# Low parts of the down weights by adding DMA transfers, and one order of the SBUF pools

## The chip, the cores and the metric

One core of one Trainium2 chip runs the whole program. The metric is device time in microseconds of one execution; a profile of one execution gives the times of single instructions. The engines are TensorE (PE, with its weight loads as PEld), VectorE (DVE), ScalarE (ACT), GpSimd (POOL) and SyncE (SP). SP, ACT and POOL each issue DMA transfers from a queue of their own; sixteen DMA engines carry them.

## The reference

A decoder trunk with two layers, run for a prompt of 512 tokens and 8 sample tokens that share the weights (D = 1024, fp32):

```python
# every layer
x = x + 0.5 * swiglu_a(rmsnorm(x))
x = x + mixer(rmsnorm(x))      # layer 0: differential attention and gated linear attention
x = x + 0.5 * swiglu_b(rmsnorm(x))   # layer 1's mixer: mLSTM matrix memory
```

A SwiGLU half-step has a gate and an up projection from 1024 to 22 hidden blocks of 128 columns, the product silu(gate) * up, and a down projection back to 1024. There are four half-steps: FFN1, (even mixer), FFN2, FFN3, (odd mixer), FFN4. Besides y the program returns new keys, values and states; the change touches none of these.

## The kernel before

**Data.** x stays in SBUF as 128 partitions by 8 blocks by 520 columns and is worked on in two chunks of 256 and 264 columns. Every fp32 product is made of three matmuls on fp32r operands: `dense` (L86) multiplies high weights by high inputs (L100), high weights by low inputs (L101) and low weights by high inputs (L102). A high part is the rounded copy of a value, the low part what is left.

**Weights.** All weights lie in HBM in the order of their use, in units of eight 128x128 blocks (512 KB). `fetch` (L72) loads a unit into one of three `raw` buffers, from SP's queue, or from POOL's in the even mixer. `split` makes the two parts: ACT copies raw to `whi` (L105) and DVE subtracts, raw minus whi, to `wlo` (L106). `whi` and `wlo` have five buffers each in the half-steps, used as a ring; the mixers have rings of their own (five or seven buffers of half the size). High priority in the framework's scheduler moves the split of a unit ahead of other work. That scheduler fixes the order of instructions on every engine before the program runs.

**A half-step.** `ffn` (L243) takes the 22 hidden blocks in three groups of 8, 7 and 7. The first four of them are plain products; the others use a seven-product scheme with combined weights, whose sums DVE makes (L425). After its hidden blocks each group has a down stage: for each of the eight output blocks as many blocks of down weights as the group has hidden blocks, two chunks (`y`), and DVE's update of x by -0.5 y (L549). A group so has 8 or 7 units of down weights, and the twelve down stages of the four half-steps have 88 (of the 192 casts of whole raw units the others are for gate and up weights). In the third group of FFN1, FFN2 and FFN3 the last four output blocks run chunk by chunk, and the norm of the next step begins beside them. In the mixers `L1510` makes a row `oner`, and the projections' results are `pj`.

**Pools.** SBUF tiles come from pools that lie one above the other and are opened anew for every half-step and mixer; a tile that lies where an older one lay waits until that one has been read for the last time. After a mixer (FFN2, FFN4) the pool `ffn` (xb, the hidden values hh and hl, and others) lies below the weights' pool `whl`; in FFN1 and FFN3 `whl` lies below. Both mixers open their own `whl` first, at the bottom. `xb` holds combined inputs of the seven products and is read for the last time by the last product ahead of the third down stage.

Of the kernel before, what the change touches and what calls it, by code (L numbers as in the profile page):

```python
# [15 lines left out]
P = 128  # L16
D = 1024
KT = 8
# [37 lines left out]
class Net:  # L56
    def __init__(self, nc, tc, t):
        self.nc, self.tc, self.t = nc, tc, t
        self.wq = nc.sync
        self.queue, self.due, self.rate, self.todo, self.side = [], 0.0, STEP, [], []  # L60
        self.seek(0)
# [13 lines left out]
    def weight(self):  # L75
        nc, g = self.nc, self.wgrp
        u, s = divmod(self.wpos, UNIT)
        self.fetch(u)
        v, r = divmod(self.wpos, g)
        if self.hl[0] != v:  # L80
            raw = self.raw[1][:, (s - r) * P:(s - r + g) * P]
            hi = self.whl.tile([P, g * P], F32R, tag="whi", name="whi")
            lo = self.whl.tile([P, g * P], F32R, tag="wlo", name="wlo")
            with self.tc.high_priority(AHF if g == UNIT else AHM):
                self.split(hi, lo, raw)
            self.hl = (v, hi, lo)  # L86
        self.wpos += 1
        return self.hl[1][:, r * P:r * P + P], self.hl[2][:, r * P:r * P + P]
# [118 lines left out]
    def head_norm_steps(self, x, parts, g, s, n, per, js=range(4), y=None):  # L207
# [18 lines left out]
        for j in js:  # L226
# [3 lines left out]
            if m > 1:  # L230
                ex = self.tmp.tile([P, 3, P], F32, tag="ex", name="ex", bufs=1)
# [11 lines left out]
    def ffn(self, pos, first, last, mixed):  # L243
# [10 lines left out]
        from contextlib import ExitStack  # L254
        H = KT // 2
        n0, n1 = CH[0][1], CH[1][1]
        with ExitStack() as ctx:
            self.wgrp = UNIT

            if not mixed:  # L260
                self.whl = self.pool(ctx, "whl", WHL)
            hp = self.pool(ctx, "ffn")
            if mixed:
                self.whl = self.pool(ctx, "whl", WHL)
            pa = self.pool(ctx, "pacc", 6, space=PSUM)
            pst = self.pool(ctx, "pst", 2, space=PSUM)
            self.stat = lambda name: pst.tile([P, 512], F32, tag="st", name=name)
            xh, xl, x = self.xh, self.xl, self.x
            xb = [hp.tile([P, 3, H, n1], F32R, tag=f"xb{i}", name="xb") for i in range(2)]
            late = slice(n0, T)  # L270
            ops = {
                "x11": lambda k: (xh[:, k, :n0], xl[:, k, :n0]),
                "x21": lambda k: (xh[:, H + k, :n0], xl[:, H + k, :n0]),
                "x22": lambda k: (xh[:, H + k, late], xl[:, H + k, late]),
                "a": lambda k: (xh[:, k, late], xl[:, k, late]),
                **{n: lambda k, i=i: (xb[0][:, i, k, :], xb[1][:, i, k, :]) for i, n in enumerate("bcd")},
            }

            slots = {(0, 0): "c", (1, 0): "d", (0, 1): "x22", (1, 1): "b"} if first else \
                {(0, 0): "x11", (1, 0): "x21", (0, 1): "d", (1, 1): "x22"}  # L280

            def put(name, k, n, src):
                hi, lo = ops[name](k)
                self.split(hi[:, :n], lo[:, :n], src)
            xn = hp.tile([P, KT, T], F32, tag="hh", name="xn")
            cm = hp.tile([P, 4, H, n1], F32, tag="hl", name="cm")
            rms = [self.rms, hp.tile([P, n1], F32, tag="rms", name="rms")]

            def raw(c, ks):

                s, n = CH[c]
                for k in ks:
                    q = xn[:, k, s:s + n]
                    g = self.ng[:, self.gi, k:k + 1]
                    if c:
                        nc.scalar.activation(q, x[:, k, s:s + n], AF.Copy, scale=g)
                    else:
                        nc.vector.tensor_scalar(q, x[:, k, s:s + n], g, None, ALU.mult)
                    put(slots[k // H, c], k % H, n, q)

            def norm(c, ks):
                s, n = CH[c]
                for k in ks:
                    q = xn[:, k, s:s + n]
                    r = rms[c]
                    if first:
                        nc.vector.tensor_tensor(out=q, in0=q, in1=r, op=ALU.mult)
                        if c == 0:
                            put("x21" if k >= H else "x11", k % H, n, q)
                    else:  # L310
                        nc.vector.scalar_tensor_tensor(q, x[:, k, s:s + n], self.ng[:, self.gi, k:k + 1], r,
                                                       ALU.mult, ALU.mult)
                        if c == 1:
                            put(slots[k // H, 1], k % H, n, q)

            def scale(c):
                r = self.rn
                self.evict(rms[c], self.spread(lambda b: r[:, b:b + 1], c))

            steps = []  # L320

            def begin():

                lo, hi = slice(0, n0), slice(n0, n1)
                x11, x21 = xn[:, :H, :n0], xn[:, H:, :n0]
                x12, x22 = xn[:, :H, late], xn[:, H:, late]
                a, c, b, d = [cm[:, i] for i in range(4)]
                if first:
                    self.x_stats(0)
                    yield  # L330
                    scale(0)
                    yield
                    raw(1, range(KT))
                    yield
                    for k in range(KT):
                        self.sq_add(1, k)
                    yield
                self.norm_stats(1)
                if not first:
                    norm(0, range(H))  # L340
                yield
                scale(1)
                if first:
                    norm(0, range(H))
                    yield
                norm(1, range(H))
                yield
                norm(1, range(H, KT))
                yield
                nc.vector.tensor_tensor(out=a[:, :, lo], in0=x11, in1=x12[:, :, lo], op=ALU.subtract)  # L350
                nc.vector.tensor_scalar(a[:, :, hi], x12[:, :, hi], -1.0, None, ALU.mult)
                self.split(xh[:, :H, late], xl[:, :H, late], a)
                yield
                norm(0, range(H, KT))
                yield
                nc.vector.tensor_tensor(out=c, in0=x22, in1=x12, op=ALU.subtract)
                nc.vector.scalar_tensor_tensor(b[:, :, lo], c[:, :, lo], -1.0, x11, ALU.mult, ALU.subtract)
                nc.vector.tensor_scalar(b[:, :, hi], c[:, :, hi], -1.0, None, ALU.mult)
                yield
                nc.vector.scalar_tensor_tensor(d[:, :, lo], b[:, :, lo], -1.0, x21, ALU.mult, ALU.subtract)  # L360

            def then():

                a, c, b, d = [cm[:, i] for i in range(4)]
                self.split(xb[0][:, 0], xb[1][:, 0], b)
                yield
                if first:
                    self.split(xh[:, H:, late], xl[:, H:, late], xn[:, H:, late])
                    yield
                self.split(xb[0][:, 1], xb[1][:, 1], c)  # L370
                yield
                self.split(xb[0][:, 2, :, :n0], xb[1][:, 2, :, :n0], d[:, :, :n0])

            def step():
                if steps and next(steps[0], 0) == 0:
                    steps.pop(0)

            def early(f, w, c):

                s, n = CH[c]  # L380
                rhs = lambda k: tuple(q[:, :n] for q in ops[slots[k // H, c]](k % H))
                g, u = bank("g"), bank("u")
                self.dense(g[:, :n], w[:KT], rhs)
                step()
                self.dense(u[:, :n], w[KT + H:] + w[KT:KT + H], rhs)
                step()
                h = f.h[:, s:s + n]
                if first:
                    r = rms[c]
                    v = small("v")[:, :n]  # L390
                    nc.vector.tensor_tensor(out=h, in0=g[:, :n], in1=r, op=ALU.mult)
                    nc.scalar.activation(h, h, AF.Silu)
                    nc.vector.tensor_tensor(out=v, in0=u[:, :n], in1=r, op=ALU.mult)
                    nc.vector.scalar_tensor_tensor(h, v, -1.0, h, ALU.mult, ALU.mult)
                else:
                    nc.scalar.activation(h, g[:, :n], AF.Silu)
# [1451 lines left out]
```

## Time and profile before

| | us |
|---|---|
| median of 3 runs | 2218.35 (2216.83 to 2223.81) |
| profiled execution | 2217.88 |
| its span in the trace | 2216.1 |
| mean granted clock of TensorE | 0.993 of full speed |

The stages in the trace: FFN1 to 375 us, the even mixer to 798, FFN2 to 1158, FFN3 to 1522, the odd mixer to 1850, FFN4 to the end. The down stages stand, among others, at 100 to 148 and 2057 to 2099. In a row of a timeline the square bracket gives how long the engine had been idle before, and what ended that.

### The profile page before, as it was taken

To read this page: it belongs to the slowest core of one execution; us is meant where nothing else is said; L and a number is where in the kernel's file an instruction comes from. 1 tells how busy PE (TensorE), PEld (TensorE's weight loads), DVE (VectorE), ACT (ScalarE), POOL (GpSimd) and SP (SyncE) were. 2 spreads that over 40 slices of the span, in tenths; PEclk is the share of its full clock that TensorE was granted. 3 is DMA by queue.
4 is the path that set the end of the run, shared out by engine and by line. 5 is a ranking of instruction groups with operands and counts; after the bars stand their busy time and mean duration, and the time that the engine had idled before them with its cause. 6 is when DMAs were issued, how large, how long until landed. Compare 5 with 4: busy or idle time off the path is not lost. (4 is left out here: it accounts for less than half of the span.)

```text
span 2216.1 us, 45677 instructions
## 1 busy us (share of the span) xinstructions
PE 2171.6 (98%) x18340; PEld 2047.6 (92%) x18340; DVE 1511.2 (68%) x3161; ACT 1010.1 (46%) x1932; POOL 47.5 (2%) x112
## 2 busy tenths in 40 slices
PE   8999999999999999999999999999999999999999
PEld 8999999876777799999999999999999899999999
DVE  8858585544486697585868767677655678758583
ACT  6526263334523355253635445353555555526261
POOL 0000001000000100000000000000000000000000
PEclk9999999999999999999999999999999999999999
DMA  5323234478677743233223323232545464323322
GB/s 183 105 67 123 78 96 152 137 257 272 235 262 244 236 144 102 81 98 102 83 96 99 124 69 123 71 109 96 157 150 158 149 194 150 96 86 92 110 77 87
DMA packets 107019, 296.30 MB, mean 134 GB/s; under 512 B 12129, under 2 KB 16786, under 8 KB 106678
## 3 DMA queue, kind: packets, MB, share of 16 engines
q1 hardware_dynamic: 93504, 254.91, 36.0%
q0 software_dynamic: 7536, 25.42, 3.6%
q10 hardware_dynamic: 5766, 13.05, 1.6%
q8 instruction: 144, 2.36, 0.4%
q14 instruction: 69, 0.57, 0.1%
HBM read 276.22 MB, written 17.11 MB: 132 GB/s over the span
## 5 line engine op out<-in xcount | busy, mean ns | idle before, releaser
L105 ACT CAST whi<-raw 128x512 fp32r<-128x512 f32 (+1 forms) x440 | 351.1, 806 | 426.5 <-PE y L101 167.1
L106 DVE TENSOR_TENSOR wlo<-raw,whi 128x512 fp32r<-128x512 f32 (+1 forms) x440 | 401.5, 920 | 146.4 <-ACT whi L105 134.8
L100 PE MATMUL y<-hh,whi 128*128 128x256 f32 (+1 forms) x1408 | 398.1, 283 | 0.0
L101 PE MATMUL y<-hl,whi 128*128 128x256 f32 (+1 forms) x1408 | 398.0, 283 | 0.0
L102 PE MATMUL y<-hh,wlo 128*128 128x256 f32 (+1 forms) x1408 | 396.8, 282 | 0.0
L101 PEld LDWEIGHTS y<-hl,whi 128*128 128x128 f32 x1408 | 265.2, 188 | 1.0 <-DVE hl L106 0.7
L100 PEld LDWEIGHTS y<-hh,whi 128*128 128x128 f32 x1408 | 264.7, 188 | 0.8
L102 PEld LDWEIGHTS y<-hh,wlo 128*128 128x128 f32 x1408 | 264.8, 188 | 0.0
L100 PE MATMUL pj<-xh,whi 128*128 128x264 f32 (+1 forms) x896 | 260.8, 291 | 4.1 <-DVE oner L1510 1.5
L102 PE MATMUL pj<-xh,wlo 128*128 128x264 f32 (+1 forms) x896 | 255.1, 285 | 3.0 <-DVE wlo L106 2.9
L101 PE MATMUL pj<-xl,whi 128*128 128x264 f32 (+1 forms) x896 | 256.0, 286 | 0.0
L100 PE MATMUL A<-xb,whi 128*128 128x264 f32 (+1 forms) x864 | 249.3, 290 | 0.6
L101 PE MATMUL A<-xb,whi 128*128 128x264 f32 (+1 forms) x864 | 244.2, 284 | 0.0
L102 PE MATMUL A<-xb,wlo 128*128 128x264 f32 (+1 forms) x864 | 243.0, 284 | 0.1
L105 ACT CAST whi<-graw 128x1024 fp32r<-128x1024 f32 x144 | 147.6, 1049 | 162.7 <-PE y L101 104.1
L549 DVE SCALAR_TENSOR_TENSOR x<-y,x 128x256 f32<-128x256 f32 (+1 forms) x192 | 81.8, 426 | 180.7 <-PE y L102 180.2
L106 DVE TENSOR_TENSOR wlo<-graw,whi 128x1024 fp32r<-128x1024 f32 x144 | 172.4, 1218 | 30.6 <-ACT whi L105 30.6
L100 PEld LDWEIGHTS pj<-xh,whi 128*128 128x128 f32 x896 | 170.5, 190 | 20.1 <-issue 11.2
L102 PEld LDWEIGHTS pj<-xh,wlo 128*128 128x128 f32 x896 | 170.3, 190 | 4.5 <-DVE wlo L106 3.4
L101 PEld LDWEIGHTS pj<-xl,whi 128*128 128x128 f32 x896 | 170.4, 190 | 3.9 <-issue 3.3
L100 PEld LDWEIGHTS A<-xb,whi 128*128 128x128 f32 x864 | 162.5, 188 | 9.2 <-DVE c L476 2.8
L100 PE MATMUL E<-xh,whi 128*128 128x264 f32 x576 | 163.7, 284 | 1.6 <-ACT whi L105 1.6
(468 smaller groups left out, 5093.1 us busy)
## 6 DMA issues: line engine op xcount, KB each, us to landing
raw<-w SPq DMA_DIRECT2D x240, 512.0 KB, 3.6
graw<-w SPq DMA_DIRECT2D x72, 512.0 KB, 4.3
kt<-ckt SPq DMA_DIRECT2D x128, 256.0 KB, 4.4
vtile<-cv SPq DMA_DIRECT2D x128, 256.0 KB, 4.0
raw<-w POOLq DMA_DIRECT2D x40, 512.0 KB, 4.7
cs<-sc SPq DMA_DIRECT2D x16, 512.0 KB, 6.4
kb<-kqd SPq DMA_DIRECT2D x16, 512.0 KB, 6.6
o_cs<-cs ACTq DMA_DIRECT2D x16, 512.0 KB, 5.6
```

The source lines that it names most:

```text
L100: nc.tensor.matmul(ps, lhsT=wh, rhs=xh, start=(ends[0] and i == ks[0]), stop=False, skip_group_check=open_)
L101: nc.tensor.matmul(ps, lhsT=wh, rhs=xl, start=False, stop=False, skip_group_check=open_)
L102: nc.tensor.matmul(ps, lhsT=wl, rhs=xh, start=False, stop=(ends[1] and i == ks[-1]), skip_group_check=open_)
L105: self.nc.scalar.copy(out=hi, in_=src)
L106: self.nc.vector.tensor_tensor(out=lo, in0=src, in1=hi, op=ALU.subtract)
L549: nc.vector.scalar_tensor_tensor(xs, y[:, :n], -0.5, xs, ALU.mult, ALU.add)
```

## The change

In the down stages the low part is made in another way: ACT copies raw to `whi`, ACT writes the negated `whi` to `wlo`, and a DMA transfer from POOL's queue adds the unit from HBM onto it. DVE's subtraction is left out there. All other weights are split as before.

All half-steps use one order of pools: `xb` at the bottom, then `whl`, then `ffn`. FFN2 and FFN3, which follow each other, share the pools and so the ring of weight buffers. Two constant rows move from a pool that lives through the program to the even mixer's own, with their memset.

```diff
@@ weight()
             with self.tc.high_priority(AHF if g == UNIT else AHM):
-                self.split(hi, lo, raw)
+                if g == UNIT and self.wadd:
+                    nc.scalar.copy(out=hi, in_=raw)
+                    nc.scalar.activation(lo, hi, AF.Copy, scale=-1.0)
+                    nc.gpsimd.dma_start(out=lo, in_=self.t["w"][u].bitcast(F32R), accum_op=ALU.add)
+                else:
+                    self.split(hi, lo, raw)
@@ ffn()
-    def ffn(self, pos, first, last, mixed):
+    def ffn(self, steps):
         with ExitStack() as ctx:
             self.wgrp = UNIT
-            if not mixed:
-                self.whl = self.pool(ctx, "whl", WHL)
+            xp = self.pool(ctx, "ffnx")
+            self.whl = self.pool(ctx, "whl", WHL)
             hp = self.pool(ctx, "ffn")
-            if mixed:
-                self.whl = self.pool(ctx, "whl", WHL)
...
+            for pos, first, last, nxt in steps:
+                self.nxt, self.nxk = nxt
+                self.half_step(pos, first, last, xp, hp, pa)
@@ half_step(), the former body of ffn()
-            xb = [hp.tile([P, 3, H, n1], F32R, tag=f"xb{i}", name="xb") for i in range(2)]
+        xb = [xp.tile([P, 3, H, n1], F32R, tag=f"xb{i}", name="xb") for i in range(2)]
...
                 self.seek((fs[0].u0 + 2 * nf) * UNIT)
+            self.wadd = True
...
+            self.wadd = False
@@ even()
             self.ev = ev = self.pool(ctx, "ev")
+            self.rows = [ev.tile([P, 384], F32, tag=f"row{c}", name="row") for c in range(2)]
+            for a in self.rows:
+                nc.gpsimd.memset(a, 1.0)
@@ head_norm_steps()
-                ex = self.tmp.tile([P, 3, P], F32, tag="ex", name="ex", bufs=1)
+                ex = self.ev.tile([P, 3, P], F32, tag="ex", name="ex")
@@ setup()
-        self.rows = [self.tmp.tile([P, 384], F32, tag=f"row{c}", name="row", bufs=1) for c in range(2)]
-        for a in [self.acc[1]] + self.rows:
-            nc.gpsimd.memset(a, 1.0)
+        nc.gpsimd.memset(self.acc[1], 1.0)
```

## Rows read from the trace of the kernel before

**Rows 1.** Page, part 1: busy time and instructions of each engine.

```profile
PE 2171.6 (98%) x18340; PEld 2047.6 (92%) x18340; DVE 1511.2 (68%) x3161; ACT 1010.1 (46%) x1932; POOL 47.5 (2%) x112
```

**Rows 2.** Windows of the down stages, one and the sum of twelve.

```profile
core 0: us, PE busy (x) PEld busy (x) DVE busy (x) ACT busy (x) POOL busy (x), PEclk, DMA share, GB/s
...
2057.00:2099.00 42.00, 42.00 (x350) 41.75 (x349) 24.19 (x40) 9.88 (x13) 0.00 (x0) 1.00 0.28 89
...
sum 525.00, PE 524.97 PEld 521.37 DVE 278.37 ACT 122.17 POOL 10.61; mean PE 43.75 PEld 43.45 DVE 23.20 ACT 10.18 POOL 0.88
```

**Rows 3.** Window of a last product before its down stage.

```profile
2042.00:2058.00 16.00, 15.89 (x132) 15.68 (x131) 13.84 (x22) 10.72 (x19) 0.00 (x0) 1.00 0.41 142
```

**Rows 4.** Timeline of PE, FFN1 to the even mixer: start, us, instruction.

```profile
374.61 0.28 PE L102 MATMUL y<-hh,wlo 128*128 128x264 f32 x1
375.63 0.39 PE L100 MATMUL pj<-xh,whi 128*128 128x256 f32 x1 [0.75 <-ACT whi L105]
375.86 0.28 PE L101 MATMUL pj<-xl,whi 128*128 128x256 f32 x1
379.00 0.58 PE L102 MATMUL pj<-xh,wlo 128*128 128x256 f32 x1 [2.86 <-DVE wlo L106]
```

**Rows 5.** Timelines of ACT and DVE there.

```profile
374.97 0.61 ACT L105 CAST whi<-raw 128x512 fp32r<-128x512 f32 x1
...
377.57 0.43 DVE L106 TENSOR_TENSOR xl<-xt,xh 128x256 fp32r<-128x256 f32 x1
...
378.26 1.29 DVE L106 TENSOR_TENSOR wlo<-raw,whi 128x512 fp32r<-128x512 f32 x2
```

**Rows 6.** Windows there, columns as in rows 2.

```profile
378.00:384.00 6.00, 5.00 (x23) 4.99 (x24) 5.46 (x23) 0.91 (x3) 1.07 (x2) 0.50 0.89 282
...
385.00:386.00 1.00, 1.00 (x10) 0.88 (x8) 0.00 (x0) 0.85 (x3) 0.00 (x0) 1.00 0.98 401
```

**Rows 7.** Timeline of PE, the waits at the other three borders.

```profile
1159.41 0.39 PE L100 MATMUL g<-xh,whi 128*128 128x256 f32 x1 [1.04 <-ACT whi L105]
...
1160.36 0.39 PE L100 MATMUL u<-xh,whi 128*128 128x256 f32 x1 [0.45 <-ACT whi L105]
...
1523.12 0.39 PE L100 MATMUL pj<-xh,whi 128*128 128x256 f32 x1 [0.56 <-ACT whi L105]
...
1525.09 0.39 PE L100 MATMUL pj<-xh,whi 128*128 128x256 f32 x1 [1.46 <-DVE oner L1510]
...
1851.56 0.39 PE L100 MATMUL g<-xh,whi 128*128 128x256 f32 x1 [1.13 <-ACT whi L105]
...
1852.51 0.39 PE L100 MATMUL u<-xh,whi 128*128 128x256 f32 x1 [0.45 <-ACT whi L105]
```

**Rows 8.** Groups by shape: busy us, mean ns, idle before.

```profile
L106 DVE TENSOR_TENSOR wlo<-raw,whi 128x1024 fp32r<-128x1024 f32 x192 | 232.7, 1221 | 41.4 <-ACT whi L105 41.1
...
L105 ACT CAST whi<-raw 128x1024 fp32r<-128x1024 f32 x192 | 199.2, 1047 | 235.5 <-PE y L101 129.4 <-DVE raw L425 60.3 <-issue 16.5
...
L1462 ACT ACTIVATE cs<-cs,pdb 128x512 f32<-128x512 f32 x32 | 22.5, 720 | 42.5 <-DMA cs<-sc 38.9 <-issue 3.5
```

**Rows 9.** DMA queues, issues with us to landing, and POOL's group of issues.

```profile
q1 hardware_dynamic: 93504, 254.91, 36.0%
...
raw<-w POOLq DMA_DIRECT2D x40, 512.0 KB, 4.7
...
o_k<-kn POOLq DMA_DIRECT2D x1, 1040.0 KB, 8.8
...
L72 POOL DMA_DIRECT2D raw<-w x40 | 21.2, 529 | 622.1 <-DMA raw<-w 331.0 <-DVE wlo L106 237.8 <-ACT xh L105 11.9
```

**Rows 10.** Timelines of ACT and PE around the start of FFN4's second down stage.

```profile
2047.59 2.00 ACT L105 CAST whi<-raw 128x1024 fp32r<-128x1024 f32 x2
...
2049.81 0.37 ACT L577 ACTIVATE c<-A 128x256 f32<-128x256 f32 x1
...
2054.71 1.05 ACT L105 CAST whi<-raw 128x1024 fp32r<-128x1024 f32 x1 [0.21 <-PE B L101]
...
2057.80 0.28 PE L102 MATMUL y<-hh,wlo 128*128 128x256 f32 x1
```

More of the change, by code (lines that the diff above doesn't have):

```diff
@@ L240, in head_norm_steps @@
             nc.vector.scalar_tensor_tensor(xs, xs, g(j), bc[:, :n], ALU.mult, ALU.mult)
-    def ffn(self, pos, first, last, mixed):
-        nc, tc = self.nc, self.tc
+    def ffn(self, steps):
         from contextlib import ExitStack
-        H = KT // 2
-        n0, n1 = CH[0][1], CH[1][1]
         with ExitStack() as ctx:
             self.wgrp = UNIT
-            if not mixed:
-                self.whl = self.pool(ctx, "whl", WHL)
+            xp = self.pool(ctx, "ffnx")
+            self.whl = self.pool(ctx, "whl", WHL)
             hp = self.pool(ctx, "ffn")
-            if mixed:
-                self.whl = self.pool(ctx, "whl", WHL)
             pa = self.pool(ctx, "pacc", 6, space=PSUM)
@@ L267, in ffn @@
             self.stat = lambda name: pst.tile([P, 512], F32, tag="st", name=name)
-            xh, xl, x = self.xh, self.xl, self.x
-            xb = [hp.tile([P, 3, H, n1], F32R, tag=f"xb{i}", name="xb") for i in range(2)]
[L270 to L287, printed above, removed]
@@ L289, in raw @@
-            def raw(c, ks):
-                s, n = CH[c]
[L292 to L296, printed above, removed]
-                    else:
[L298 to L396, printed above, removed]
-                    nc.vector.scalar_tensor_tensor(h, u[:, :n], -1.0, h, ALU.mult, ALU.mult)
@@ L399, in unit @@
-            def unit(u, gate):
-                raw = (hp.tile([P, UNIT * P], F32, tag="graw", name="graw", bufs=2) if gate else
-                       self.wraw.tile([P, UNIT * P], F32, tag="raw", name="raw"))
-                self.wq.dma_start(out=raw, in_=self.t["w"][u])
-                return raw
-            def parts(src, n, names):
-                tag = "" if n == 2 else "u"
-                hi = self.whl.tile([P, n * H * P], F32R, tag=f"whi{tag}", name="whi", bufs=None if n == 2 else 2)
-                lo = self.whl.tile([P, n * H * P], F32R, tag=f"wlo{tag}", name="wlo", bufs=None if n == 2 else 2)
-                self.split(hi, lo, src)
-                return {name: [(hi[:, i * P:i * P + P], lo[:, i * P:i * P + P]) for i in range(b * H, b * H + H)]
-                        for b, name in enumerate(names)}
@@ L414, in weights_gate @@
-            def weights_gate(f):
-                f.g = unit(f.u0, True)
-                with tc.high_priority(AHF):
-                    f.w = parts(f.g, 2, ("g1", "g2"))
-            def weights_rest(f):
-                B = H * P
-                f.u = unit(f.u0 + 1, False)
-                g1, g2, u2, u1 = f.g[:, :B], f.g[:, B:], f.u[:, :B], f.u[:, B:]
-                def add(x, y):
-                    nc.vector.tensor_tensor(out=x, in0=x, in1=y, op=ALU.add)
-                with tc.high_priority(AHF):
-                    f.w |= parts(u2, 1, ("u2",))
-                    add(u2, u1)
-                    add(u1, g1)
-                    f.w |= parts(f.u, 2, ("s1", "s3"))
-                    add(g1, u2)
-                    add(g2, g1)
-                    f.w |= parts(f.g, 2, ("s2", "s4"))
@@ L435, in ffn @@
-            class Hidden:
-                def __init__(self, u0):
-                    self.u0 = u0
-            def bank(name):
-                return pa.tile([P, 512], F32, tag="acc", name=name)
-            def small(name):
-                return hp.tile([P, n1], F32, tag=name, name=name, bufs=2)
-            def product(kind, f, j):
-                w, v = {"p1": ("g1", "x11"), "p2": ("g2", "x21"), "q5": ("s1", "a"), "q6": ("s2", "b"),
-                        "p7": ("s3", "c"), "p3": ("s4", "x22"), "p4": ("u2", "d")}[kind]
-                n = n0 if kind in ("p1", "p2", "p4") else n1
-                new = kind in ("p1", "p2", "q5")
-                if kind == "p1":
-                    f.A = bank("A")
-                elif kind == "p2":
-                    f.B = bank("B")
-                elif kind == "q5":
-                    f.E = bank("E")
-                ps = f.B if kind == "p2" else f.E if kind in ("q5", "p3") else f.A
-                self.dense(ps[:, :n], f.w[w], lambda k: tuple(q[:, :n] for q in ops[v](k)), ends=(new, True),
-                           open_=kind != "p2")
-                if kind == "p1":
-                    f.c1 = small("c1")
-                    self.evict(f.c1[:, :n0], ps[:, :n0])
-                elif kind == "p2":
-                    g = f.c1[:, :n0]
-                    nc.vector.tensor_tensor(out=g, in0=ps[:, :n0], in1=g, op=ALU.add)
-                    nc.scalar.activation(g, g, AF.Silu)
-                elif kind == "q5":
-                    f.c5 = small("c5")
-                    self.evict(f.c5, ps[:, :n1])
-                elif kind == "q6":
-                    f.v = small("v")
-                    self.evict(f.v, ps[:, :n1])
-                elif kind == "p3":
-                    nc.vector.tensor_tensor(out=f.v, in0=ps[:, :n1], in1=f.v, op=ALU.add)
-                    nc.scalar.activation(f.v, f.v, AF.Silu)
-                elif kind == "p7":
-                    nc.vector.tensor_tensor(out=f.c5, in0=ps[:, :n1], in1=f.c5, op=ALU.add)
-                    nc.vector.tensor_tensor(out=f.v, in0=f.v, in1=f.c5, op=ALU.mult)
-                    self.split(hh[:, j, late], hl[:, j, late], f.v)
-                elif kind == "p4":
-                    g = f.c1[:, :n0]
-                    nc.vector.tensor_tensor(out=g, in0=ps[:, :n0], in1=g, op=ALU.mult)
-                    self.split(hh[:, j, :n0], hl[:, j, :n0], g)
-                step()
@@ L485, in ffn @@
-            u0 = pos // UNIT
-            groups = []
-            for nf in GROUPS:
-                groups.append([Hidden(u0 + 2 * j) for j in range(nf)])
-                u0 += 3 * nf
-            leads = groups[0][:LEAD]
-            self.seek(pos)
-            if first:
-                self.fetch(pos // UNIT)
-                self.x_load(0, KT)
-                raw(0, range(KT))
-            steps.append(begin())
-            i = 0
-            while i < LEAD:
-                fs = leads[i:i + (2 if i == 0 else 1)]
-                ws = [self.weights(2 * KT) for _ in fs]
-                if first and i == 0:
-                    self.x_load(KT, 2 * KT)
-                for f in fs:
-                    f.h = hp.tile([P, T], F32, tag="h", name="h", bufs=LEAD)
-                if i == 0 and not first:
-                    step()
-                for c in range(2):
-                    for f, w in zip(fs, ws):
-                        early(f, w, c)
-                i += len(fs)
@@ L511, in ffn @@
-            while steps:
-                step()
-            steps.append(then())
-            for gi, (nf, fs) in enumerate(zip(GROUPS, groups)):
-                order = []
-                for j in range(LEAD if gi == 0 else 0, nf):
-                    order += [("gate", j), ("rest", j), ("p1", j), ("q5", j)] + [("p4", j - 1)] * (j > (LEAD if gi == 0 else 0))
-                    order += [("q6", j), ("p2", j), ("p3", j), ("p7", j)]
-                order.append(("p4", nf - 1))
-                hh = hl = None
-                for kind, j in order:
-                    if hh is None and kind in ("p7", "p4"):
-                        hh = hp.tile([P, max(GROUPS), T], F32R, tag="hh", name="hh")
-                        hl = hp.tile([P, max(GROUPS), T], F32R, tag="hl", name="hl")
-                        if gi == 0:
-                            for i, f in enumerate(leads):
-                                self.split(hh[:, i], hl[:, i], f.h)
-                    if kind == "gate":
-                        weights_gate(fs[j])
-                    elif kind == "rest":
-                        weights_rest(fs[j])
-                    else:
-                        product(kind, fs[j], j)
-                while steps:
-                    if next(steps[0], 0) == 0:
-                        steps.pop(0)
-                self.seek((fs[0].u0 + 2 * nf) * UNIT)
-                end = gi == len(GROUPS) - 1
-                def hrhs(c):
-                    s, n = CH[c]
-                    return lambda k: (hh[:, k, s:s + n], hl[:, k, s:s + n])
-                def down(d, c, w):
-                    s, n = CH[c]
-                    y = bank("y")
-                    self.dense(y[:, :n], w, hrhs(c))
-                    xs = x[:, d, s:s + n]
-                    nc.vector.scalar_tensor_tensor(xs, y[:, :n], -0.5, xs, ALU.mult, ALU.add)
-                    if end:
-                        if last:
-                            if c == 1:
-                                nc.sync.dma_start(out=self.t["o_y"][:, d, :], in_=x[:, d, :])
-                        else:
-                            self.sq_add(c, d)
-                if end:
-                    self.gi = self.nxt
-                lag = 4 if (end and not last) else 0
-                for d in range(KT - lag):
-                    w = self.weights(nf)
-                    down(d, 0, w)
-                    down(d, 1, w)
-                if lag:
-                    ahead = self.norm_lead() if self.nxk == "ffn" else self.norm_ahead(1)
-                    w = [self.weights(nf) for _ in range(lag)]
-                    for c in range(2):
-                        for i in range(lag):
-                            down(KT - lag + i, c, w[i])
-                            if c:
-                                next(ahead, None)
-                    for _ in ahead:
-                        pass
@@ L1657, in run @@
             self.setup(ctx)
-            for i, st in enumerate(stages):
-                last = i == len(stages) - 1
-                self.nxt, self.nxk = (None, None) if last else (stages[i + 1][1], stages[i + 1][0])
-                if st[0] == "ffn":
-                    self.ffn(st[2], i == 0, last, i > 0 and stages[i - 1][0] != "ffn")
-                else:
-                    getattr(self, st[0])(*st[2:])
-                    if last:
+            nxt = [(st[1], st[0]) for st in stages[1:]] + [(None, None)]
+            last = len(stages) - 1
+            i = 0
+            while i <= last:
+                self.nxt, self.nxk = nxt[i]
+                if stages[i][0] == "ffn":
+                    j = i
+                    while i < last and stages[i + 1][0] == "ffn":
+                        i += 1
+                    self.ffn([(stages[k][2], k == 0, k == last, nxt[k]) for k in range(j, i + 1)])
+                else:
+                    getattr(self, stages[i][0])(*stages[i][2:])
+                    if i == last:
                         self.nc.sync.dma_start(out=self.t["o_y"], in_=self.x)
+                i += 1
             self.x_close()
```

279 lines of the change are left out of this document (added).

## The prediction

> **What bounds the kernel now.** I read the engines' shares first: PE 98% of the span, no other engine above 68% [rows 1]. So only two kinds of edit can move the time: one that makes PE idle, and one that removes an idle stretch of PE. Next come the windows. The change rewrites the twelve down stages, so their table tells what there is to win in them: in 525 us of them PE is busy for 524.97, DVE for 278 and ACT for 122 [rows 2]. No time is to be won there; 42 us hold 350 matmuls, 0.12 us each, so a unit (8 blocks, 2 chunks, 3 products, 48 matmuls) lasts 5.76 us. The last product before a down stage costs PE a tenth of a microsecond at most: 15.89 of 16, with DVE at 13.84 and ACT at 10.72, the fullest place of both [rows 3]. Then PE's timeline at the borders of half-steps and mixers: there PE does stand still, and always for the first weights of the next stage or what follows from them [rows 4, 7]. That is what the new order of pools touches.
>
> **The borders (order of pools): a gain.** A matmul follows the one before by 0.12 us; where PE waited, the step between starts is the shown idle time plus 0.27, so each wait costs its idle time plus 0.15.
>
> *FFN1 to the even mixer.* The last y starts at 374.61, the first pj at 375.63, its second product at 375.86 and its low-part product at 379.00: (1.02 - 0.12) + (3.14 - 0.12) = 3.9 us [rows 4]. ACT casts the first mixer weights only at 374.97, directly after the last y, because the mixer's weight buffers lie where FFN1's weights and hidden values lay; DVE is then late with the low part as it has the norm's work in its queue [rows 5]. After this idle time the granted clock is 0.50, the lower level, from 378 to 384, and back to 1.00 at 385: 23 matmuls took 5.00 us, 0.217 each instead of 0.12, another 2.2 us [rows 6]. Together 6.1. With the new order these buffers lie over xb, last read by the last product, a whole down stage earlier, so cast and low part can be made ahead. What is late next is the norm: its last xl ends at 378.00, and the eighth block's second product would want it 22 matmuls after 374.73, at 377.4: 0.6 stays. Gain 5.5.
>
> *FFN2 to FFN3* now share one ring of weight buffers. Idle 1.04 + 0.45 [rows 7], plus 0.15 each: 1.8. I take it all, as the ring's next buffer comes free with every down unit.
>
> *FFN3 to the odd mixer.* Idle 0.56 for the cast and 1.46 for DVE's oner, which is no weight [rows 7]. The first goes (0.7); of the second (1.6) I take half, since the mixer's first low parts are then no longer in DVE's queue beside it. 1.5.
>
> *Odd mixer to FFN4.* Idle 1.13 + 0.45, 1.9 with the restarts [rows 7]. The buffers will lie over early-released tiles, not over yl, which the last matmul reads; but casts are then queued between the projection's own work on ACT, so I take 1.2.
>
> *Even mixer to FFN2* waits for other things; nothing. The moved memset of the rows is two short POOL instructions; nothing.
>
> Sum 5.5 + 1.8 + 1.5 + 1.2 = 10.0. Bounds: 12.1 if every wait goes (6.1 + 1.8 + 2.3 + 1.9), 3 if only about a quarter does, because the raw transfer or DVE's norm takes each wait's place.
>
> **The adds: what is removed.** 88 subtractions of 1221 ns, 107 us of DVE [rows 8]. DVE was idle for nearly half of these stages [rows 2], so this is worth nothing by itself.
>
> **The adds: what is added.** On ACT 88 negations. The nearest row is the cast of the same shape, 1047 ns; a scaled activation of half the size took 720 [rows 8] where the cast took 0.61 us [rows 5], so 1.05 to 1.24. I take 1.05, since it too is one pass over 128x1024: 92 us, ACT 122 to about 214 of 525 in these stages. On POOL 88 issues of 529 ns, 47 us on an engine that is busy for 47 in all [rows 1, 9]. An add waits for its negation, and POOL takes its queue in order: behind it stand only the next adds, and at the end of FFN1 the even mixer's first raw loads, which wait for buffers themselves [rows 9] and are needed a down stage later; so a late add delays nothing but its own unit. SP's raw loads wait for less than before, since a raw buffer is free after ACT's cast instead of after DVE's subtraction. On the DMA engines 88 transfers of 512 KB that read, add and write. No row shows such a transfer.
> Latency: a plain 512 KB transfer from POOL's queue lands after 4.7 us, one of 1040 KB after 8.8 [rows 9]. That gives 4.7 below and 8.7 above (two plain passes in a row, roughly the larger one). I take 6.3: the plain one and one more pass at the engines' rate. A pass is worked out from SP's queue: 254.91 MB in 36.0% of 2216.1 us is 320 GB/s, 1.64 us for 512 KB [rows 9].
> Engine time: with raw's one pass (0.28 of 5.76 is 1.6 [rows 2]) 4.1 us per unit are left, 2.5 passes. One pass is the lower bound; three (read, read, write, one after the other) the upper. I take the middle, two, 3.3 us: hidden, with the engines busy for about 0.85 of a down stage.
> The Trainium skill, "Collectives: The Full Stack", section "The bandwidth ceiling: the fold count and why AG ≠ RS ≠ AR", says that an add on the way costs no cycles of its own but needs two source reads, and so runs at half the rate (32.35 against 62.28). No run here shows it; by that rule the add would take an estimated 3.3 us here and the sum would stay as it is.
>
> **The first unit of a down stage.** Units later on have time: the third's cast starts at 2054.71 [rows 10] and it is used two units after the first, at 2069: 14.6 us, less 2.1 on ACT, less 6.3. The first has least. Its cast and the second's run from 2047.59 to 2049.59; its low part is read at 2057.80 [rows 10]; the other eleven stages look alike. With negations between, the first negation ends at 2049.7 (cast, negation) or 2050.6 (both casts first). The add lands at 2056.0 to 2056.9 by my value, in time by 0.9; by the upper bound at 2059.3, 1.5 late. Then the evictions on ACT behind these: c<-A at 2049.81 starts 2.1 later, and PE can want its bank. PE has other banks and products, so I take 0.25 us per stage, between 0 and the full 2.1: 12 x 0.25 = 3.0, at most 25. Below zero is possible too: DVE, at 13.84 of 16 here, loses two subtractions per transition, and PE's 0.11 us of idle time could go, 12 x 0.11 = 1.3 us.
>
> **Sum.** Profiled execution 2217.9 (span 2216.1 and 1.8 around it) - 10.0 + 3.0 = 2210.9. The median of the runs is 2218.35, half a microsecond more; I say 2211.
>
> **Rivals.**
> *Late at each transition:* the adds land after the first use, or ACT's evictions hold PE up, 0.5 to 1.6 us each: 12 x 0.5 to 1.6 gives 6 to 19, so 2207.9 + 6 to 19: 2214 to 2227. For it: 0.9 us of slack by my value, and a full ACT and DVE exactly there [rows 3, 10]. Against: PE has the whole of two more products in between.
> *The add is slow, and the kernel slower:* if an add takes the 16 engines more than 4.1 us (2.5 passes), units can't arrive at PE's rate. At three passes a unit takes 4 x 1.64 = 6.56 instead of 5.76 us: 88 x 0.80 = 70, time 2208 + 70 = 2278; at four, 88 x 2.44 = 215, 2423. For it: nothing in the trace prices a transfer that reads its target. Against: rows of plain transfers leave 0.72 of the engines free.
> *The borders don't gain:* buffers free earlier, but casts keep their place in ACT's order, or raw and DVE's norm are last: 3 gained and 3 lost, 2218 (2215 to 2221). For it: an engine's order is fixed beforehand, and two of the four waits come partly from DVE. Against: the casts follow directly on the last y, so what held them was the buffer.
> *More is gained:* all 12.1, nothing at the transitions, and some of DVE's lateness at FFN starts goes: 2201 to 2207.
>
> **How the numbers follow.** Forecast (2207 to 2213) 0.40; late at transitions 0.22; slow add 0.15; borders don't gain 0.10; more gained 0.13. A measurement of this kernel tells 0.3% from no change, 6.65 us: 2211.7 to 2225.0 is "same". The forecast lies with 0.34 below and 0.06 in it; more gained is faster; late is 0.15 same and 0.07 slower; borders 0.08 and 0.02; slow add 0.15 slower. Faster 0.34 + 0.13 = 0.47; same 0.06 + 0.15 + 0.08 = 0.29; slower 0.07 + 0.02 + 0.15 = 0.24. Range 2204 to 2230: it leaves out the slow add (0.15), and the ends of more gained and late (0.05). The likeliest case's own range is 2207 to 2213.
>
> **What would show it.** Borders: whi casts for the first mixer and FFN weights ahead of the last y; no idle 2.86 before pj's low product; clock 1.00 through 378 to 384. Adds: DVE near 1404, ACT near 1102 and POOL near 94 us; the POOL add's landing between 4.7 and 8.7; DMA share of a down stage near 0.85. Transitions: no wait of y L102 on a DMA. I am wrong if y L102 waits on wlo's DMA inside the down stages (slow add), if it does for the first unit alone, or if new waits stand at 375, 1159, 1523 and 1851.

## The result: slower by 0.9%

| | us |
|---|---|
| before, median of 6 runs | 2219.01 |
| changed, median of 6 runs | 2239.32 (2236.33 to 2247.56) |
| ratio, with its 95% interval | 1.0092 [1.0078, 1.0105] |
| profiled execution of the changed kernel | 2247.56, span 2245.8, clock 0.989 |

The forecast was 2211, range 2204 to 2230: the measured time lies above it, and it moved the other way. The profiled execution is the slowest of the six; its span is 29.7 us longer than the one of before.

The page's first part, and its rows on queues and issues (packets, MB and share of 16 engines; KB and us to landing):

```profile
PE 2176.8 (97%) x18340; PEld 2054.8 (91%) x18340; DVE 1410.5 (63%) x3073; ACT 1090.1 (49%) x2020; POOL 123.7 (6%) x200
...
q1 hardware_dynamic: 93504, 254.91, 35.0%
q0 software_dynamic: 20208, 71.56, 14.7%
...
wlo<-w POOLq DMA_DIRECT2D x88, 512.0 KB, 9.0
...
raw<-w POOLq DMA_DIRECT2D x40, 512.0 KB, 4.6
```

The work moved as counted: DVE lost 101 us against [rows 1], ACT gained 80, POOL 76, and PE does the same matmuls. The new row is the add's landing, 9.0 us in the median. PE's waits (us in all, times, longest) name it:

```profile
PE y L109 <- DMA wlo<-w: 20.2, 13, 3.6
...
PE ss L161 <- DVE acc L130: 7.4, 2, 3.9
...
PE A L107 <- ACT c L590: 1.3, 8, 0.2
```

The first row has thirteen waits: one at the first unit of each of the twelve down stages (0.3 to 2.7 us, 16.6 in all) and one at FFN1's last unit (3.6). With 0.15 for each restart they cost 22.2 us. After the four longest (2.1 to 3.6 us) the granted clock falls to 0.50, the lower level, for part of the windows below. One of three windows of that kind, and FFN1's (columns as in [rows 2]):

```profile
1014.00:1018.00 4.00, 4.00 (x22) 4.00 (x22) 0.89 (x3) 0.93 (x2) 0.87 (x1) 0.57 1.06 287
...
368.00:374.00 6.00, 4.97 (x29) 4.97 (x30) 1.27 (x3) 0.44 (x2) 0.53 (x1) 0.72 0.31 107
```

(1 - 0.57) x 4 is 1.7 us, three times, and (1 - 0.72) x 6 another 1.7: 6.8. Together 29.0 of the 29.7. All the rest, borders and mixers with their gains and losses, sums to under 1 us.

**The start of a down stage**, the place of [rows 10]. ACT, POOL, SP and PE there:

```profile
2075.04 1.99 ACT L88 CAST whi<-raw 128x1024 fp32r<-128x1024 f32 x2
2076.94 2.00 ACT L89 ACTIVATE wlo<-whi 128x1024 fp32r<-128x1024 f32 x2
```

```profile
2078.28 1.81 POOL L90 DMA_DIRECT2D wlo<-w  x2 [85.92 <-ACT wlo L89]
```

```profile
2075.16 2.23 SPq L73 DMA_DIRECT2D raw<-w  x3
2077.51 0.36 SPq L413 DMA_DIRECT2D graw<-w  x1
```

```profile
2085.15 0.28 PE L107 MATMUL y<-hh,whi 128*128 128x256 f32 x1
2085.27 0.28 PE L108 MATMUL y<-hl,whi 128*128 128x256 f32 x1
2087.14 0.38 PE L109 MATMUL y<-hh,wlo 128*128 128x256 f32 x1 [1.59 <-DMA wlo<-w]
```

From the first cast to the first use of its low part there are 10.4 us (to 2085.39, where PE would have used it); before there were 10.2. Casts and negations take 3.2 to the issue at 2078.28, and the transfer lands 8.8 later, at 2087.09. The window over the stretch shows why (the share is a sum of packet times and can pass 1.00; read it as full):

```profile
2076.00:2100.00 24.00, 22.25 (x183) 21.83 (x182) 5.82 (x14) 12.26 (x21) 4.31 (x5) 1.00 1.02 263
```

Each cast frees a raw buffer, so SP sends four 512 KB loads just ahead of the first two adds. Three more loads and three more adds follow by 2090, and for 24 us the sixteen engines are full. The Trainium skill, "DMA: Bandwidth & Descriptors", section "Issuing engines are not separate DMA queues", says that transfers of all issuing engines run on the same sixteen and interleave; these rows agree, with loads from SP's queue and adds from POOL's in one full stretch.

### The profile page after: what moved, and what is told of

The parts are those of the page before. It is cut to its first block, busy times and chain, and to the rows that moved or that the text cites. A ratio compares the mean times of both kernels' runs of the same rounds, so it can differ in the third digit from the quotient of the medians.

```text
span 2245.8 us, 45941 instructions
## 1 busy us (share of the span) xinstructions
PE 2176.8 (97%) x18340; PEld 2054.8 (91%) x18340; DVE 1410.5 (63%) x3073; ACT 1090.1 (49%) x2020; POOL 123.7 (6%) x200
## 3 DMA queue, kind: packets, MB, share of 16 engines
q0 software_dynamic: 20208, 71.56, 14.7%
## 5 line engine op out<-in xcount | busy, mean ns | idle before, releaser
L112 ACT CAST whi<-raw 128x512 fp32r<-128x512 f32 (+1 forms) x352 | 261.2, 746 | 404.1 <-PE y L108 109.7
L113 DVE TENSOR_TENSOR wlo<-raw,whi 128x512 fp32r<-128x512 f32 (+1 forms) x352 | 295.6, 845 | 189.8 <-ACT whi L112 178.5
```

The lines of the kernel that those rows point to most:

```text
L112: self.nc.scalar.copy(out=hi, in_=src)
L113: self.nc.vector.tensor_tensor(out=lo, in0=src, in1=hi, op=ALU.subtract)
```

## The experiments

**The two halves.** The adds with the old pools (`weight()` and the `wadd` flags alone):

> The adds alone: the order of pools and the rows' memset are those of before. Theory A (the add of the first unit of each down stage lands after PE wants it): y's low product waits for wlo's DMA at 12 stages, about 20 us in all, as in the changed kernel; median 2234 to 2246 us. Rival P (the order of pools does the harm, since high-priority splits of the next stage's weights get ahead of the norm on DVE): waits for wlo's DMA under 8 us in all, median 2214 to 2226 us.

Median 2236.23, ratio 1.0072 [1.0054, 1.009]; y waits 14.9 us for the adds, at the twelve first units. And the pools alone:

```diff
-            self.wadd = True
```

> The order of pools alone: every low part by DVE's subtraction. Theory A: no wait of y on a DMA; the border of FFN1 and the even mixer gains some 4 us, and the norm's waits at 389 and 806 (accumulator of squares, 3.9 and 3.5 us in the changed kernel) give about as much back; median 2212 to 2222 us. Rival P: 2228 to 2240 us.

2219.55, ratio 0.9999 [0.9989, 1.0009]. So the adds carry the loss (16 of the 20 us by themselves), and the pools, from which I forecast 10 us, give nothing. The other 4 us come with both halves together: only then does FFN1's last unit wait. Theory A stands, P falls.

**The add's own price.**

```diff
-                    nc.gpsimd.dma_start(out=lo, in_=self.t["w"][u].bitcast(F32R), accum_op=ALU.add)
+                    nc.gpsimd.dma_start(out=lo, in_=self.t["w"][u].bitcast(F32R))
```

> As the changed kernel, but the transfer from POOL's queue writes the unit over the negated part instead of adding it (the low parts of the down weights are therefore wrong). Theory A1 (the add's own passes make it late): landing about 5 to 6 us instead of 9.0, y's waits for wlo under 6 us in all, median 2214 to 2226 us. Rival A2 (ACT's order, two casts and then two negations, and the bytes in the queue make it late, whatever the transfer does with them): landing 7.5 us or more, waits of 12 us or more, 2230 us or more.

2219.61, ratio 0.9997 [0.9984, 1.001], with the same work on ACT and the same 46 MB more from HBM as in the changed kernel. Its rows on the queue and the issue, and then what PE still waits for it:

```profile
q0 software_dynamic: 20208, 71.56, 10.1%
...
wlo<-w POOLq DMA_DIRECT2D x88, 512.0 KB, 6.0
```

```profile
PE y L109 <- DMA wlo<-w: 0.7, 2, 0.5
```

So with a plain transfer in its place the waits are gone, and theory A1 stands: neither ACT's longer chain nor the bytes make PE wait by themselves. But the plain transfers also load the engines less, so this run does not tell the add's own time from the full engines. At the twelve first units the plain transfer landed after 6.8 us (median), in a stretch that was full as well; the add there took 8.7.

The engines' time comes from q0's share, less the 3.6% of before (79.8 us): 10.1% of 2221.4 is 224.4, so 144.6 / 88 = 1.64 us per plain load; 14.7% of 2245.8 is 330.1, so 250.3 / 88 = 2.84 us per add. An add is 1.7 passes. The issue on POOL takes 0.53 us for the plain load and 0.86 for the add. By the measured 2.84 an add runs at 0.58 of the plain rate. The Trainium skill, "Collectives: The Full Stack", section "The bandwidth ceiling: the fold count and why AG ≠ RS ≠ AR", measured half the rate in a reduce-scatter among four ranks. The estimate of 3.3 us that the prediction worked out by it is somewhat too long for this transfer.

**Which units.** The first three units of a down stage by ACT and DVE, then the first alone (`wu` counts the units of a stage):

```diff
-                if g == UNIT and self.wadd:
+                if g == UNIT and self.wadd and self.wu > 3:    # then: > 1
```

> As the changed kernel, but the first three units of each down stage are split by ACT and DVE as before (36 of 88); 52 are made by adds. Theory A: no waits of y on wlo's DMA of over 0.5 us; the median equals that of the pools alone within 5 us, 2212 to 2224. Rival L (46 MB more on the DMA engines or 92 us more on ACT slow everything, at whatever unit): over 10 us of the loss stays, 2230 us or more.

2218.65, ratio 0.9993 [0.9981, 1.0005]; one wait for an add is left, 0.3 us.

> As the changed kernel, but the first unit of each down stage, 12 of 88, is split by ACT and DVE; 76 are made by adds. Theory A: the second unit has 5.8 us more, so the twelve waits go, and at most 4 us stay (FFN1's last unit); median 2217 to 2224 us. Rival Q (the queue of adds is late as such): the wait moves to the second unit, 8 us or more of it, 2227 us or more.

2223.02, ratio 1.0005 [0.9993, 1.0017]. Its one wait for an add:

```profile
PE y L111 <- DMA wlo<-w: 4.4, 1, 4.4
```

This is FFN1's last unit, at 365; the twelve are gone. So 12 of 88 units carry the loss of the down stages, and rival L falls. For the last unit the trace of this run shows its cast at 351.77, between casts for the mixer, only some 9 us ahead of its use, and two mixer loads on POOL's queue just before its add; it landed after 10.3 us. Which of these decides was not tried apart. With the old pools it did not wait.

**ACT's chain or the engines' queue.** The negation from raw, ahead of the cast:

```diff
-                    nc.scalar.copy(out=hi, in_=raw)
-                    nc.scalar.activation(lo, hi, AF.Copy, scale=-1.0)
+                    nc.scalar.activation(lo, raw, AF.Copy, scale=-1.0)
                     nc.gpsimd.dma_start(out=lo, ...)
+                    nc.scalar.copy(out=hi, in_=raw)
```

> As the changed kernel, but ACT writes the negated part first, straight from raw, then starts the cast of the high part; the add waits for one instruction instead of two (or three, as the second unit's cast stood between). Theory A (the chain of ACT and the add ends late for the first unit, by 0.3 to 2.7 us): the first add of a stage is issued 1.8 us earlier, against the first use; of the 16.7 us that twelve first units cost, 2 us stay (0.9, 0.3 and 0.6), beside the 3.6 of FFN1's last unit; median 2220 to 2228 us. Rival Q (the first add is late because the transfers of units behind it share the engines, so an earlier issue only moves the queue): first waits of 10 us or more stay, 2231 us or more.

2256.81, ratio 1.0154 [1.0132, 1.0176]: a miss, against theory A's number. ACT's order at the same place, and the two waits that cost most:

```profile
2082.92 1.05 ACT L90 CAST whi<-raw 128x1024 fp32r<-128x1024 f32 x1
2083.87 2.00 ACT L88 ACTIVATE wlo<-raw 128x1024 fp32r<-128x1024 f32 x2
2085.78 1.03 ACT L90 CAST whi<-raw 128x1024 fp32r<-128x1024 f32 x1
```

```profile
PE y L107 <- ACT hh L112: 13.7, 8, 2.5
PE y L109 <- DMA wlo<-w: 13.6, 9, 2.6
```

The scheduler left the first cast in front all the same. The add went out 2.3 us after it instead of 3.2, and landed 9.7 us later instead of 8.8: at 12.0 after the cast, as in the changed kernel. Over the twelve stages the first add landed after 9.6 us in the median instead of 8.7, later by what it was issued earlier. An earlier issue only moved the queue, as rival Q had it. Alone this does not prove it: both ACT passes now read raw, so the loads moved too (the third goes out 1.6 us behind the first add instead of 1.2 ahead). And the rearranged ACT now makes the last hidden values (hh) late, a second wait of the same size.

**More load at that place.** A plain load of 512 KB per down stage, from SP's queue, into a tile nobody reads:

```diff
                     nc.scalar.copy(out=hi, in_=raw)
+                    self.wu += 1
+                    if self.wu == 1:
+                        nc.scalar.copy(out=self.spare[:, :8], in_=raw[:, :8])   # second form: in_=hi[:, :8]
+                        nc.sync.dma_start(out=self.spare, in_=self.t["w"][u])
...
+            self.spare = hp.tile([P, UNIT * P], F32, tag="spare", name="spare")
```

> As the changed kernel, with one plain load of 512 KB more per down stage (12 in all, into a tile that nobody reads), issued from SP's queue right after the cast of the stage's first unit. Theory A2 (the 16 engines are full at the start of a down stage, 0.94 to 1.07 of them from 2076 to 2100 in the changed kernel, so the first add waits for its share of them): the first add of a stage lands 1 to 1.6 us later, y's waits for wlo's DMA grow by 10 to 18 us, median 2249 to 2262 us. Rival D (the delay of 8.7 us is the add's own, however full the engines are): landing and waits stay as they are, 2234 to 2244 us.

2238.10, ratio 1.0084 [1.0061, 1.0107]: no loss was added (the first adds land after 8.5 us, the waits sum to 15.7). But the tile waited for raw alone, so the load went out 20 us ahead of the add and had landed long before it: 6 MB more cost nothing there, and the question stayed open. With the load tied to the cast:

> As the run before with an extra plain load of 512 KB per down stage into a tile that nobody reads, but the load waits for the cast of the stage's first unit (there it waited for the raw data alone, and went out 20 us before the first add). Theory A2 (the engines are full at the start of a down stage and the first add waits for its share): the first add lands 1 to 1.6 us later than in the changed kernel (8.65 us median), y's waits for wlo's DMA grow from 20 to 30 us or more, median 2249 to 2262 us. Rival D (the 8.65 us are the add's own): landing and waits as in the changed kernel, 2234 to 2244 us.

2267.25, ratio 1.0224 [1.0202, 1.0247]. The load goes out 1.2 us ahead of the first add. At the place shown above for the changed kernel, the issues of the load and of the first two adds, then the first add's time to landing, in the changed kernel and here, and PE's waits here:

```profile
2091.75 0.33 SPq L92 DMA_DIRECT2D spare<-w  x1
...
2092.98 1.80 POOL L94 DMA_DIRECT2D wlo<-w  x2 [85.64 <-ACT wlo L93]
```

```profile
wlo<-w POOLq DMA_DIRECT2D x1, 512.0 KB, 8.8
...
wlo<-w POOLq DMA_DIRECT2D x1, 512.0 KB, 10.0
```

```profile
PE y L113 <- DMA wlo<-w: 32.1, 13, 4.4
```

Over the twelve stages the first add lands after 9.6 us (median) instead of 8.7, just under what theory A2 asked for, and PE waits 12 us more, as it asked. The time lies 28 us above the changed kernel's, beyond A2's range. The lower clock is part of it: 0.985 of 2263.8 us loses 34 us, 0.989 of 2245.8 loses 25. ACT's small copy is not the cause, since the run before had it too. Theory A2 stands, D falls: the landing depends on how full the engines are. Holding SP's loads back until the first add has landed was not tried.

**Where the pools' gain went.** In the pools alone, PE and DVE at the end of FFN1, to be held against [rows 4, 5]:

```profile
375.29 0.28 PE L109 MATMUL pj<-xh,wlo 128*128 128x256 f32 x1
379.51 0.80 PE L161 MATMUL ss<-ones,acc 128*128 128x1 f32 x3 [3.94 <-DVE acc L130]
```

```profile
379.02 0.43 DVE L130 TENSOR_TENSOR acc<-acc,sq 128x264 f32<-128x264 f32 x1 [0.31 <-ACT sq L120]
```

The first three pj follow the last y without a gap: the weights are there. Then PE's fixed order has ss, the sum of squares for the second chunk's norm, and DVE finishes that sum only at 379.45. Before, the same ss started at 380.01, hidden behind the wait for the low part. Half a microsecond is won of six, and the lower clock follows as before (0.55 from 378 to 384). If so, DVE's order is what to change:

```diff
-                nc.vector.scalar_tensor_tensor(xs, y[:, :n], -0.5, xs, ALU.mult, ALU.add)
...
+                with tc.high_priority(AHX if end and not last and c else 0):   # AHX = 400; in project() likewise
+                    nc.vector.scalar_tensor_tensor(xs, y[:, :n], -0.5, xs, ALU.mult, ALU.add)
+                    if end and not last:
                         self.sq_add(c, d)
```

> The order of pools alone (no adds), and the update of x and its sum of squares for the second chunk get a higher priority in the last down outputs of a half-step and in the mixers' output projections, so that DVE makes them ahead of the norm of the first chunk and of the weights' low parts. Theory N (with the pools changed, the wait for the first weights is replaced by the wait for the sum of squares, 3.9 us at 379 and 3.0 at 801): these two waits shrink under 1.5 us each, and with them the lower clock after 379; median 2209 to 2216 us. Rival M (the chain to the second chunk's inputs, or low parts that are now late, ends the wait instead): 2216 to 2224 us.

2215.95, ratio 0.998 [0.9966, 0.9993]. PE's wait at that place, and the window from 378 to 384 in the pools alone and here:

```profile
376.84 0.38 PE L162 MATMUL ss<-ones,acc 128*128 128x1 f32 x2 [0.47 <-DVE acc L131]
```

```profile
378.00:384.00 6.00, 4.49 (x21) 4.49 (x22) 2.96 (x19) 0.42 (x1) 0.00 (x0) 0.55 0.72 244
...
378.00:384.00 6.00, 6.00 (x47) 5.23 (x45) 4.59 (x24) 2.60 (x9) 0.00 (x0) 1.00 0.85 310
```

3.9 us became 0.5, and the clock stays at 1.00 from 378 to 384. Before FFN2 1.9 of 3.0 stay, more than theory N allowed. The same priority without the pools:

> The kernel before (its order of pools, no adds) with the same higher priority for the update of x and its sum of squares. Theory N: there PE waits for the first weights, not for the sum, so nothing moves by over 2.5 us: 2216 to 2222 us. Rival: the priority is worth something by itself, 2215 us or less, or costs where the low parts then come later, 2223 us or more.

2221.63, ratio 1.0009 [1.0000, 1.0018]. The time is as theory N had it, its reason is not. At the end of FFN1 PE's waits did change:

```profile
376.54 0.38 PE L101 MATMUL pj<-xh,whi 128*128 128x256 f32 x1 [0.70 <-ACT whi L106]
377.77 0.83 PE L155 MATMUL ss<-ones,acc 128*128 128x1 f32 x6 [0.73 <-DVE acc L124]
379.88 0.58 PE L103 MATMUL pj<-xh,wlo 128*128 128x256 f32 x1 [0.87 <-DVE wlo L107]
```

They sum to 2.3 us instead of 3.6. In return the wait for ss before FFN2 grew from 0.46 to 2.08; where the rest of the gain went was not traced. Neither edit wins alone; together they do. Without the mixers' projections:

> The order of pools and the higher priority, but this only in the last down outputs of the half-steps, not in the mixers' output projections. Theory N: the gain at the end of FFN1 (3.9 us and the lower clock after it) stays, the waits before FFN2 are again 3.0 and 1.1 instead of 1.9 and 1.4; 2213 to 2219 us. Rival: the gain came from the projections, 2218 us or more.

2215.02, ratio 0.9968 [0.9957, 0.9979]. The gain at the end of FFN1 stays (a wait of 0.47 us, clock 1.00); the wait for ss before FFN2 is 2.4, not 3.0. And with the adds from the fourth unit on:

> The order of pools, adds from the fourth unit of each down stage on, and the higher priority for x and its sum of squares. If 64 us less work on DVE is worth nothing by itself, the time is that of the pools with prompt squares, 2212 to 2219 us; if DVE's backlog at the borders still counts, 2 us or more under it, 2214 or less.

2212.89, ratio 0.9969 [0.9958, 0.998]. The three runs with pools and priority are 0.2 to 0.3% faster than the kernel before, clear of noise; their intervals overlap, so whether the projections or the adds add anything is not told apart.

## Why the prediction was wrong

The profiled span was forecast 7 us shorter and came out 29.7 longer. The adds cost 29.0 instead of 3.0, and everything else lost 0.7 instead of gaining 10.0.

- *What bounds the kernel*, PE and its few idle stretches: right. The losses and gains read here are idle time of PE or the lower clock after it.
- *Landing of the first add*: this step failed. I took 6.3 us, a plain landing (4.7) and one more pass, as if the transfer met engines that are free for 0.72 of the time; waiting for full engines was put at nothing. That share [rows 2] is a mean over the down stage, and the first unit doesn't live in the mean. The casts free the raw buffers there, so three or four loads go out in the 3 us ahead of the first add; that SP's loads would go out sooner stood in the prediction, but only as a gain. The landing was 8.7 (median of twelve firsts). A plain transfer from POOL's queue took 6.8 at the same place: by these two runs, of the 4.0 us above a plain landing, 2.0 are the full stretch, which the sum left out, and 1.9 the add, for which it had 1.6. The trace of before had the full stretch already, in the six microseconds in which the first add was to run (columns as in [rows 2]):

```profile
2049.00:2055.00 6.00, 5.89 (x49) 5.68 (x48) 4.53 (x9) 3.00 (x8) 0.00 (x0) 1.00 0.89 307
```

- *The upper bound and the rival*: my upper bound for the landing, 8.7, was the true value, and its 1.5 us late at this place came out as 1.59. Its reason, two plain passes in a row, was not the cause, so that is partly luck. The rival *late at each transition* had the mechanism. It had 0.5 to 1.6 us per stage, measured 0.3 to 2.7, and it left out the lower clock that followed the four longest waits, 6.8 us.
- *Engine time of an add*: I took two passes, 3.3 us, hidden; measured 2.84, with the plain load 4.5 of a unit's 5.76. The slow add did not come: but for FFN1's last, no later unit waits.
- *ACT's evictions 0.25 us per stage*, 3.0 in all: A's eight waits on c, 1.3 us, are all that was seen.
- *The mixer's first loads stand behind the adds in POOL's queue*: wrong at FFN1's last unit, where two of them went out just ahead of its add; it waited 3.6 us.
- *Gain at the borders*, 10.0: this failed too, in what ends the wait once the weights are there. FFN1 to even: 5.5 forecast; ss was next, not xl, and 0.5 came. FFN2 to FFN3: 1.8 forecast; in the pools alone the first product on xb starts 14.4 us after the last y instead of 16.1, so right. FFN3 to odd: 1.5 forecast; 0.56 and 1.46 stay, now both for whi. Odd to FFN4: 1.2 forecast; 0.62 and 1.12 instead of 1.13 and 0.45, nothing. Even to FFN2: nothing forecast; the wait for the sum of squares grew from 0.46 to 3.00. The rival *the borders don't gain* had the result; it came true together with the late adds, and I had priced each only by itself.

## What to carry to other kernels

A mean share of the DMA engines says whether a stream of transfers keeps up, not when its first one lands: read its window over the few microseconds in which the transfer is to run, and count what else is issued in them. Give work of long latency to the units that are far ahead, and make the first ones of a stage the old way; here that took the loss away and won nothing. When a wait at a border goes, look in the engine's fixed order for the next operand that PE will want, and when it is ready in the old trace: it stands there already, hidden behind the first wait.

## What was not expected of the hardware

- A transfer that adds takes the engines 2.84 us per 512 KB where a plain one takes 1.64, and its issue on GpSimd 0.86 us instead of 0.53.
- The quickest add landed after 5.3 us (at 2103.5, with the engines' share at 0.34 in the 3 us before), the slowest after 14.0 (at 104.8, in a full stretch).
- A load of 512 KB per stage cost nothing when issued 20 us ahead of the first add, and about 28 us over twelve stages, by the medians, when issued 1.2 us ahead of it.
